# Layer 0 of a two-layer decoder: three products of 272 columns per weight chunk become products of 288, 256 and 272 columns, at changing places in memory

## The chip, the cores and the metric

The kernel runs on one core of a Trainium2 chip. Its engines each work through a queue of their own: TensorE (PE in the profile, with its weight loads as PEld), VectorE (DVE), ScalarE (ACT), GpSimd (POOL) and SyncE (SP), which issues DMAs. They wait for each other through semaphores. SBUF is the memory on the chip with 128 partitions; TensorE writes its sums to PSUM, in banks of 512 float32 columns. The metric is the device time of one execution in microseconds (us), as the median of several runs.

## The reference

256 tokens with 16 learned meta tokens in front (272 rows) go through two layers of width 2048, in float32. Cut to what matters here:

```python
h = concatenate([meta, x])                        # 272 x 2048
# layer 0
q, k, v, f = split(rms_norm(h) @ fox_w_in)        # 2048 -> 3*2048 + 16
h = h + forgetting_attention(q, k, v, cumsum(log_sigmoid(f + b))) @ fox_w_o
h = h + square(relu(rms_norm(h) @ w_up[0])) @ w_down[0]     # 2048 -> 8192 -> 2048
# layer 1
k_s, v_s = split(rms_norm(h, kv_norm) @ w_kv)     # all 272 rows
q = rms_norm(h) @ sb_w_q
h = h + stick_breaking_attention(q, k_s, v_s) @ sb_w_o
h = h + square(relu(rms_norm(h) @ w_up[1])) @ w_down[1]
return rms_norm(h, final_norm)[16:]
```

The meta tokens are needed up to the shared keys and values. From the queries of layer 1 on, only the 256 other tokens are computed.

## The kernel before

Everything is kept with the features on the partitions: `hT` is 128 partitions x 16 chunks x 272 tokens. A matrix product takes 128 x 128 weights as the stationary operand and a chunk of rows (128 features x tokens) as the moving one, in the type float32r. To keep float32's precision, both operands are split in two parts, a rounded one (`hi`) and the rest (`lo`), and three products are added up: weights-hi x rows-hi, weights-hi x rows-lo, weights-lo x rows-hi.

**Groups.** `gemm_group` (L186) makes 512 output features: 4 accumulators `acc` (one PSUM bank each, m = 0 to 3) by 4 blocks `kb` of the contraction, each with 4 chunks `kc`. A group is 4 x 16 x 3 = 192 products. For each `kb` the weights come by DMA into two tiles `raw` (L208, 512 KB each), ScalarE rounds them to `whi` (L220), VectorE subtracts to get `wlo` (L221). `whi` and `wlo` have 4 buffers each of half a block, so the splitting runs up to two blocks ahead. In the blocks 0 and 3 the products go accumulator by accumulator (12 in a row for each), in the blocks 1 and 2 half by half. At the end of block 3 a function `evac` takes each accumulator: in the projections VectorE multiplies it by the norm's factor (L377, L381), in the down and output products it adds it to `hT` (L255), in the up products it makes relu, square and split of it (L514 to L519). The next group uses the same four banks again.

**Stages.** Layer 0 has 12 groups for q, k and v (rows `a0`), 4 for the output product (`o0`), and for each of four quarters of the MLP 4 up groups (rows `m0`) and 4 down groups (rows `u0_0` to `u0_3`). Layer 1 begins with 4 groups for the queries on 256 tokens, then 8 groups for the shared keys and values on all 272 (rows `kv`); all that follows has 256 tokens. In the attention stages the small matrix products of the attention (L345 and others) are issued between the products of the groups.

**Where the rows lie.** `Split` (L119) holds `hi` and `lo` of one stage in one tile, 640 columns for each chunk. `ROWS` (L27) gives the first column of each: for 272 tokens `hi` at column 48 and `lo` at 368, for 256 tokens at 0 and 320. The tiles begin at a multiple of 64 columns (256 bytes), so that 48 and 368 are both column 48 of a stretch of 64. The weights lie at column 0 of their tiles where the rows are 272 and at column 16 where they are 256 (L212). In the layer-1 groups three products of each group are 262 columns wide instead of 256 (`wide`, L242 and L247); the six more columns are zeros and are not read.

**What sets the order.** The program is laid out by a scheduler that orders the instructions of each engine after a time model. The products of the groups are pinned one behind the other (`pinned`, L181). At the start, the first group loads the input and the weights by pieces, and takes the chunks one by one (L227).

Of the kernel before, what the change touches and what calls it, by code (L numbers as in the profile page):

```python
# [33 lines left out]
def yoco_kernel(ctx: ExitStack, tc: tile.TileContext, hT_in, gains, b_f, w_f, w_qkv0, w_o0, w_up, w_dn,  # L34
                w_kv, w_q1, w_o1, outT):
    nc = tc.nc
# [7 lines left out]
    tmp = ctx.enter_context(tc.tile_pool(name="tmp", bufs=2))  # L44
# [74 lines left out]
    class Split:  # L119


        def __init__(self, label, t0):
            n = T - t0
            self.t0 = t0
            rows = xs.tile([P, NC * XROW + 64], F32R, tag="x", name=f"x_{label}")
            hi, lo = ROWS[t0]
            rows = rows[:, hi:hi + NC * XROW].rearrange("p (c t) -> p c t", c=NC)
            d = lo - hi
            self.hi, self.lo = rows[:, :, :n], rows[:, :, d:d + n]
            if t0:  # L130

                self.wide = rows[:, :, :n + 6]
                nc.gpsimd.tensor_copy(rows[:, :, n:n + 6], pad[:, :6].unsqueeze(1).to_broadcast([P, NC, 6]))

    def split_chunk(sp, gi, c):

        g = g_sb[:, gi, c:c + 1]
        nc.scalar.activation(sp.hi[:, c], hT[:, c, sp.t0:], AF.Copy, scale=g)
        nc.vector.scalar_tensor_tensor(out=sp.lo[:, c], in0=hT[:, c, sp.t0:], scalar=g,
                                       in1=sp.hi[:, c].bitcast(F32), op0=ALU.mult, op1=ALU.subtract)  # L140

    class Norm:

# [34 lines left out]
    def gemm_matmul(*args, **kw):  # L178

        ins = nc.tensor.matmul(*args, **kw).ins  # L180
        if queued and pinned[0]:  # L181
            tc.add_manual_dep(ins, queued[0].name, mybir.DependencyInfo(mybir.DependencyClass.NoSync,
                                                                        mybir.DependencyReason.DATA))
        queued[:] = [ins]

    def gemm_group(wblk, sp, t0, evac, before={}, after={}, load_x=None):  # L186
# [4 lines left out]
        u = uid[0]  # L191
        accs = [pacc.tile([P, 512], F32, tag="acc", name=f"acc_{u}_{m}") for m in range(4)]
        n = T - t0
        for kb in range(4):
# [14 lines left out]
            parts = []  # L209
            for hf in range(2):  # L210
                whi, wlo = (wspl.tile([P, 2, 576], F32R, tag=f"w{x}", name=f"w{x}_{u}_{kb}_{hf}") for x in ("hi", "lo"))
                o = 16 if t0 else 0  # L212
                whi, wlo = whi[:, :, o:o + 512], wlo[:, :, o:o + 512]
                boxes = [(o, piece, 0, 512) for o in range(0, 2, piece)]
                if load_x is not None and kb == hf == 0:
                    boxes[:1] = [(0, 1, 0, 256), (0, 1, 256, 512)]
                for o, no, c0, c1 in boxes:
                    src = raws[hf][:, o:o + no, c0:c1]
                    hp, lp = whi[:, o:o + no, c0:c1], wlo[:, o:o + no, c0:c1]
                    on_act = nc.scalar.activation(hp, src, AF.Copy)  # L220
                    on_dve = nc.vector.tensor_tensor(out=lp, in0=src, in1=hp.bitcast(F32), op=ALU.subtract)  # L221
                parts.append((whi, wlo))
# [11 lines left out]
            for kcs, ms in runs:  # L234
                pairs = ((0, sp.hi), (0, sp.lo), (1, sp.hi))
                if t0:
                    products = [(kc, m, *pair) for pair in pairs for kc in kcs for m in ms]
                else:
                    products = [(kc, m, *pair) for m in ms for kc in kcs for pair in pairs]
                left = {m: 3 * len(kcs) for m in ms}  # L240

                wide = [(0, 0, 0), (1, 0, 1), (2, 1, 1)] if t0 else []  # L242
                for kc, m, part, x in products:
                    first, left[m] = kb == kc == 0 and left[m] == 3 * len(kcs), left[m] - 1
                    nw = n
                    if m == 3 and x is sp.hi and (kb, kc, part) in wide:
                        x, nw = sp.wide, n + 6  # L247
                    gemm_matmul(accs[m][:, :nw], parts[kc // 2][part][:, kc % 2, m * P:(m + 1) * P], x[:, 4 * kb + kc],
                                start=first, stop=kb == kc == 3 and left[m] == 0)
                if kb == 3:  # L250
                    for m in ms:
                        evac(m, accs[m][:, :n])

    def residual_add(c, acc, t0):
        nc.vector.tensor_tensor(out=hT[:, c, t0:], in0=acc, in1=hT[:, c, t0:], op=ALU.add)  # L255
# [109 lines left out]
    def put_split(sp, h, nh, t, n, src):  # L365
        hi, lo = (x[:, h:h + nh, t - sp.t0:t - sp.t0 + n] for x in (sp.hi, sp.lo))
        nc.scalar.activation(hi, src, AF.Copy)
        nc.vector.tensor_tensor(out=lo, in0=src, in1=hi.bitcast(F32), op=ALU.subtract)

    ao = Split("o0", 0)  # L370
    for g in range(4):
# [129 lines left out]
    def mlp(layer, xm, norm, t0, last_evac):  # L501
# [5 lines left out]
        for f in range(N_FF):  # L507
            u = Split(f"u{layer}_{f}", t0)
            for g in range(4):
                def evac(m, acc, g=g):  # L510
# [6 lines left out]
                    nc.scalar.activation(u.hi[:, c], u2[:, t0:], AF.Copy)  # L517
                    nc.vector.tensor_tensor(out=u.lo[:, c], in0=u2[:, t0:], in1=u.hi[:, c].bitcast(F32),
                                            op=ALU.subtract)  # L519
                gemm_group(w_up[layer, f, g], xm, t0, evac, {2: get_rstd} if f == g == 0 else {})  # L520
            for g in range(4):
                def evac(m, acc, g=g):
# [245 lines left out]
```

## Time and profile before

| | |
|---|---|
| median of 2 runs | 2295.25 us (2295.24 to 2295.26) |
| the profiled execution | 2294.73 us |
| its span, first to last instruction | 2293.0 us |
| PE busy | 2281.7 us, 19086 products |
| DVE, ACT, POOL busy | 1315.9, 1065.7, 39.8 us |
| mean granted clock of TensorE | 0.998 |

A line of the groups view names the line of the kernel, the engine, the operation, what is written and read with its shape, and the count; behind the bar stand the busy time, the mean duration of one in ns, and the idle time of the engine before it with what ended it. The duration of a product overlaps with the next one's, so what a product costs is read from the distance of starts. In the chain of waits and in the timeline, pieces that follow each other on one engine are merged: start, length, and how many.

### The profile page before, as it was taken

To read this page: it belongs to the slowest core of one execution; us is meant where nothing else is said; L and a number is where in the kernel's file an instruction comes from. 1 tells how busy PE (TensorE), PEld (TensorE's weight loads), DVE (VectorE), ACT (ScalarE), POOL (GpSimd) and SP (SyncE) were. 2 spreads that over 40 slices of the span, in tenths; PEclk is the share of its full clock that TensorE was granted. 3 is DMA by queue.
4 is the path that set the end of the run, shared out by engine and by line. 5 is a ranking of instruction groups with operands and counts; after the bars stand their busy time and mean duration, and the time that the engine had idled before them with its cause. 6 is when DMAs were issued, how large, how long until landed. Compare 5 with 4: busy or idle time off the path is not lost.

```text
span 2293.0 us, 45093 instructions
## 1 busy us (share of the span) xinstructions
PE 2281.7 (100%) x19086; PEld 2278.7 (99%) x19086; DVE 1315.9 (57%) x1834; ACT 1065.7 (46%) x1465; POOL 39.8 (2%) x65
## 2 busy tenths in 40 slices
PE   9999999999999999999999999999999999999998
PEld 9999999999999999999999999999999999999998
DVE  7666565654454455455566666666555555555555
ACT  6444444543354344344445555555544543543553
POOL 1000000000000000000000000000000000000000
PEclk9999999999999999999999999999999999999999
DMA  7544545555555555555555544456566556566563
GB/s 237 175 161 163 177 158 173 173 186 175 181 169 186 180 170 186 176 181 175 176 190 191 170 148 149 153 169 202 189 195 198 188 191 203 185 199 199 187 200 132
DMA packets 116906, 412.33 MB, mean 180 GB/s; under 512 B 13520, under 2 KB 16992, under 8 KB 116704
## 3 DMA queue, kind: packets, MB, share of 16 engines
q1 hardware_dynamic: 114560, 406.29, 53.3%
q8 instruction: 149, 2.44, 0.4%
q10 hardware_dynamic: 2144, 3.17, 0.4%
q14 instruction: 53, 0.43, 0.1%
HBM read 407.29 MB, written 2.11 MB: 179 GB/s over the span
## 4 chain that ended last, share of the span: by engine, by line
PE 99%; DVE 0%; DMA 0%; ACT 0%; SPq 0%; issue 0%; DVEq 0%; ACTq 0%
PE acc L180 96%; PE po L345 0%; PE pv L335 0%; PE ps L345 0%; PE pza L345 0%; DMA raw<-w_qkv 0%; PE po L655 0%; PE pzb L607 0%; PE ps L416 0%; PE po L483 0%; DVE ob L710 0%; PE pf L297 0%; PE pf L296 0%; PE pta L621 0%; PE pta L622 0%; PE pp L451 0%
## 5 line engine op out<-in xcount | busy, mean ns | idle before, releaser
L221 DVE TENSOR_TENSOR wlo<-raw,whi 128x1024 fp32r<-128x1024 f32 (+1 forms) x773 | 928.9, 1217 | 725.6 <-ACT whi L220 715.9
L220 ACT ACTIVATE whi<-raw 128x1024 fp32r<-128x1024 f32 (+1 forms) x773 | 797.3, 1050 | 966.7 <-PE acc L180 943.7
L180 PE MATMUL acc<-x_m,whi 128*128 128x272 f32 (+1 forms) x4096 | 643.0, 281 | 0.0
L180 PE MATMUL acc<-x_u,whi 128*128 128x272 f32 (+1 forms) x4096 | 642.5, 281 | 0.0
L180 PEld LDWEIGHTS acc<-x_m,whi 128*128 128x128 f32 x4096 | 565.9, 188 | 0.1
L180 PEld LDWEIGHTS acc<-x_u,whi 128*128 128x128 f32 x4096 | 565.7, 188 | 0.0
L180 PE MATMUL acc<-x_m,wlo 128*128 128x272 f32 (+2 forms) x2048 | 440.8, 281 | 0.0
L180 PE MATMUL acc<-x_u,wlo 128*128 128x272 f32 (+2 forms) x2048 | 440.8, 281 | 0.0
L180 PE MATMUL acc<-x_a,whi 128*128 128x272 f32 (+1 forms) x2048 | 357.9, 286 | 0.3 <-ACT whi L220 0.3
L180 PEld LDWEIGHTS acc<-x_m,wlo 128*128 128x128 f32 x2048 | 323.3, 188 | 0.0
L180 PEld LDWEIGHTS acc<-x_u,wlo 128*128 128x128 f32 x2048 | 323.3, 188 | 0.0
L180 PEld LDWEIGHTS acc<-x_a,whi 128*128 128x128 f32 x2048 | 301.5, 188 | 0.8 <-ACT whi L220 0.5
L180 PE MATMUL acc<-x_a,wlo 128*128 128x272 f32 (+2 forms) x1024 | 254.5, 286 | 0.0
L180 PE MATMUL acc<-x_kv,whi 128*128 128x272 f32 x1024 | 193.4, 288 | 0.0
L180 PEld LDWEIGHTS acc<-x_a,wlo 128*128 128x128 f32 x1024 | 175.5, 188 | 0.5 <-issue 0.5
L180 PE MATMUL acc<-x_o,whi 128*128 128x272 f32 (+1 forms) x1024 | 162.8, 282 | 0.0
L180 PEld LDWEIGHTS acc<-x_kv,whi 128*128 128x128 f32 x1024 | 160.0, 188 | 0.0
L180 PE MATMUL acc<-x_kv,wlo 128*128 128x272 f32 x512 | 146.8, 287 | 0.0
L180 PEld LDWEIGHTS acc<-x_o,whi 128*128 128x128 f32 x1024 | 142.2, 188 | 0.0
L255 DVE TENSOR_TENSOR hT<-acc,hT 128x272 f32<-128x272 f32 (+1 forms) x160 | 69.1, 432 | 81.7 <-PE acc L180 81.4
L180 PE MATMUL acc<-x_o,wlo 128*128 128x272 f32 (+2 forms) x512 | 110.9, 282 | 0.0
L180 PEld LDWEIGHTS acc<-x_kv,wlo 128*128 128x128 f32 x512 | 96.4, 188 | 0.1
(239 smaller groups left out, 1043.3 us busy)
## 6 DMA issues: line engine op xcount, KB each, us to landing
raw<-w_up SPq DMA_DIRECT2D x256, 512.0 KB, 4.4
raw<-w_dn SPq DMA_DIRECT2D x256, 512.0 KB, 4.5
raw<-w_qkv SPq DMA_DIRECT2D x92, 512.0 KB, 3.7
raw<-w_o SPq DMA_DIRECT2D x64, 512.0 KB, 4.3
raw<-w_kv SPq DMA_DIRECT2D x64, 512.0 KB, 3.7
raw<-w_q SPq DMA_DIRECT2D x32, 512.0 KB, 4.5
fk<-f_dram ACTq DMA_DIRECT2D x4, 544.0 KB, 4.7
raw<-w_qkv SPq DMA_DIRECT2D x7, 256.0 KB, 4.5
```

The source lines that it names most:

```text
L180: ins = nc.tensor.matmul(*args, **kw).ins
L220: on_act = nc.scalar.activation(hp, src, AF.Copy)
L221: on_dve = nc.vector.tensor_tensor(out=lp, in0=src, in1=hp.bitcast(F32), op=ALU.subtract)
L255: nc.vector.tensor_tensor(out=hT[:, c, t0:], in0=acc, in1=hT[:, c, t0:], op=ALU.add)
```

## The change

It changes the groups with 272 rows, that is all of layer 0 and the shared keys and values: 56 groups of 96.

- Each chunk of rows is laid out as 16 columns `meta`, then the 272 columns of `hi`, and further on the 272 columns of `lo`. `copy_meta` copies the first 16 columns of `lo` (those of the meta tokens) to `meta`, on GpSimd.
- The three products become: B, weights-hi x (`meta` and `hi`), 288 columns; A, weights-hi x `lo` without its first 16 columns, 256 columns; C, weights-lo x `hi`, 272 columns. B writes the columns 0 to 288 of the accumulator, A the columns 32 to 288, C the columns 16 to 288. The sum for the meta tokens is then in two parts, and ahead of each `evac` ScalarE copies the columns 0 to 16 and VectorE adds them to the columns 16 to 32.
- `PLACES` gives for each stage the column, within a stretch of 64, at which B and A begin (C begins 16 behind B). `form` gives for each group the column at which `whi` and `wlo` begin, and the order of A, B and C.
- The layer-1 groups with 256 rows keep their products and places.

```diff
-ROWS = {0: (48, 368), M: (0, 320)}
+ROWS = {M: (0, 320)}
+PLACES = {"a0": (0, 0), "o0": (32, 0), "m0": (48, 0), "u0_0": (0, 0), "u0_1": (48, 48), "u0_2": (0, 48),
+          "u0_3": (16, 0), "kv": (48, 32)}
+FOUR = [(0, 0, "BAC"), (16, 16, "BAC"), (0, 16, "BAC"), (16, 0, "BAC")]
+def form(u):
+    o = (0, 16, 32, 48)
+    if u <= 12:
+        return [(0, 0), (16, 16), (32, 32), (48, 48), (0, 16), (0, 32), (16, 0), (16, 32), (32, 0), (32, 16), (48, 0),
+                (0, 48)][u - 1] + ("BAC",)
+    if u <= 16:
+        return [(0, 0, "BAC"), (16, 16, "BAC"), (0, 0, "ACB"), (16, 16, "ACB")][u - 13]
+    if u <= 48:
+        f, g = divmod(u - 17, 8)
+        if g < 4:
+            return o[f], o[g], "BAC"
+        return [(0, 0, "ABC"), (0, 0, "BCA"), (0, 0, "CBA"), (16, 16, "ABC")][g - 4] if f == 0 else FOUR[g - 4]
+    if 53 <= u <= 60:
+        return ([*FOUR, (32, 32, "BAC"), (48, 48, "BAC"), (0, 48, "BAC"), (48, 0, "BAC")])[u - 53]
+    return 16, 16, ""
...
-            hi, lo = ROWS[t0]
+            hi, lo = ROWS[t0] if t0 else PLACES[label]
+            if not t0:
+                while lo < hi + n + 2 * M:
+                    lo += 64
+                lo -= M
...
+                self.meta, self.hi, self.lo = rows[:, :, :M], rows[:, :, M:M + n], rows[:, :, d:d + n]
+                self.form = {"A": (0, rows[:, :, d + M:d + n], 2 * M, M + n), "B": (0, rows[:, :, :M + n], 0, M + n),
+                             "C": (1, self.hi, M, M + n)}
...
+    def copy_meta(sp, c, n=1):
+        if sp.t0 == 0:
+            nc.gpsimd.tensor_copy(sp.meta[:, c:c + n], sp.lo[:, c:c + n, :M])
...
-                o = 16 if t0 else 0
-                whi, wlo = whi[:, :, o:o + 512], wlo[:, :, o:o + 512]
+                o1, o2, order = form(u)
+                whi, wlo = whi[:, :, o1:o1 + 512], wlo[:, :, o2:o2 + 512]
...
+                if not t0:
+                    for m in ms:
+                        for kc in kcs:
+                            for x in ("BAC" if kb == kc == 0 else order):
+                                part, rows, c0, c1 = sp.form[x]
+                                left[m] -= 1
+                                gemm_matmul(accs[m][:, c0:c1], parts[kc // 2][part][:, kc % 2, m * P:(m + 1) * P],
+                                            rows[:, 4 * kb + kc], start=kb == kc == 0 and x == "B",
+                                            stop=kb == kc == 3 and left[m] == 0)
+                    products = []
...
-                        evac(m, accs[m][:, :n])
+                        acc = accs[m][:, :n]
+                        if not t0:
+                            acc = accs[m][:, M:M + n]
+                            meta = tmp.tile([P, M], F32, tag="meta", name=f"meta_{u}_{m}")
+                            nc.scalar.copy(meta, accs[m][:, :M])
+                            nc.vector.tensor_tensor(out=acc[:, :M], in0=acc[:, :M], in1=meta, op=ALU.add)
+                        evac(m, acc)
```

`u` counts the groups in the order in which they run: 1 to 12 for q, k and v, 13 to 16 for the output product, 17 to 48 for the MLP (in eights, four up and four down), 49 to 52 for the queries of layer 1, 53 to 60 for the shared keys and values. `copy_meta` is called where a chunk's `hi` and `lo` are made: in `split_chunk`, in `put_split` for the meta tokens of the attention's output, and in the evacuation of the up products.

More of the change, by code (lines that the diff above doesn't have):

```diff
@@ L140, in split_chunk @@
                                        in1=sp.hi[:, c].bitcast(F32), op0=ALU.mult, op1=ALU.subtract)
+        copy_meta(sp, c)
     class Norm:
@@ L251, in gemm_group @@
                     for m in ms:
-                        evac(m, accs[m][:, :n])
+                        acc = accs[m][:, :n]
+                        if not t0:
+                            acc = accs[m][:, M:M + n]
[3 more added lines that the diff above has]
+                        evac(m, acc)
     def residual_add(c, acc, t0):
@@ L368, in put_split @@
         nc.vector.tensor_tensor(out=lo, in0=src, in1=hi.bitcast(F32), op=ALU.subtract)
+        if sp.t0 == t == 0 and n == M:
+            copy_meta(sp, h, nh)
     ao = Split("o0", 0)
@@ L519, in evac @@
                                             op=ALU.subtract)
+                    copy_meta(u, c)
                 gemm_group(w_up[layer, f, g], xm, t0, evac, {2: get_rstd} if f == g == 0 else {})
```

5 lines of the change are left out of this document (3 added, 2 removed).

## The prediction

> **What bounds the kernel now.** I read the page first (busy shares, slices, chain), then the chain of waits stretch by stretch, then the groups with shapes kept apart.
>
> ```profile
> span 2293.0 us, 45093 instructions
> PE 2281.7 (100%) x19086; PEld 2278.7 (99%) x19086; DVE 1315.9 (57%) x1834; ACT 1065.7 (46%) x1465; POOL 39.8 (2%) x65
> ...
> PEclk9999999999999999999999999999999999999999
> ...
> PE 99%; DVE 0%; DMA 0%; ACT 0%; SPq 0%; issue 0%; DVEq 0%; ACTq 0%
> ...
> L220 ACT ACTIVATE whi<-raw 128x1024 fp32r<-128x1024 f32 (+1 forms) x773 | 797.3, 1050 | 966.7 <-PE acc L180 943.7
> ```
>
> TensorE is busy for the whole span at full clock, the chain that ends last is 99% TensorE, and ScalarE, which makes the weights ready, waits 943.7 us for TensorE to give buffers back, not the other way round. So the time is the number of products times the distance from one start to the next. That distance stands in the chain, in two undisturbed stretches, the first of layer 0 (272 columns) and the second of layer 1 (256 columns, three of 192 with 262):
>
> ```profile
> 440.00 740.12 PE acc L180 x6001
> ...
> 1599.92 680.63 PE acc L180 x6000
> ```
>
> 740.12 / 6001 = 123.3 ns for 272 columns, 680.63 / 6000 = 113.4 ns for 256. Sixteen columns fewer are worth 9.9 ns, 0.62 ns a column, while the average over all 256 is 0.44 ns. Were the distance a fixed part and a part per column, 256 columns would leave no fixed part to speak of but a negative one (113.4 - 256 x 0.62 = -45 ns). So the distance is not linear; something steps up between 256 and 272. That is what the change can gain from, with the same 816 columns in three products.
>
> What the steps are worth is not constant either. The same products come in a second rhythm after a disturbance:
>
> ```profile
> 1195.80 1.11 PE L180 MATMUL acc<-x_a,wlo 128*128 128x256 f32 x8
> 1196.75 1.99 PE L180 MATMUL acc<-x_a,whi 128*128 128x256 f32 x16
> ...
> 70.63 0.42 PE L180 MATMUL acc<-x_a,whi 128*128 128x272 f32 x2
> ...
> 71.01 0.42 PE L180 MATMUL acc<-x_a,whi 128*128 128x272 f32 x2
> ...
> 71.39 0.42 PE L180 MATMUL acc<-x_a,whi 128*128 128x272 f32 x2
> ```
>
> From 1195.80 to 1196.75 eight products of 256 (the last of them 262) take 0.95 us, 118.8 ns each, and three products of 272 take 0.38 us from 70.63 to 71.01 and again to 71.39, 126.7 ns each. At the same sizes and places the distance is thus 113.4 or some 118.5, 123.3 or 126.7, with no wait that the profile shows. A product has a good and a bad rhythm, 3.4 to 5 ns apart.
>
> **The change part by part.** The groups with 272 rows are 56 x 192 = 10752 products, 3584 triples of 3 x 123.3 = 370.0 ns, together 1326 us. The 7680 products of layer 1 with 256 rows keep size, place and order and are costed at nothing; their cover is that no row of theirs is touched.
>
> *The triple.* C (272) stays between 123.3 and 126.7 ns. A (256) lies between 113.4 and 118.8. For B (288) the nearest rows are the attention's products of that width:
>
> ```profile
> 1496.45 0.13 PE pta L623
> 1496.58 0.14 PE pta L624
> 1496.72 0.13 PE ptb L626
> 1496.85 1.39 PE acc L180 x12
> 1498.23 0.23 PE po L345 x2
> ...
> L180 PE MATMUL acc<-x_m,whi 128*128 128x272 f32 x2048 | 379.3, 287 | 0.0
> ...
> L180 PE MATMUL acc<-x_m,whi 128*128 128x256 f32 x2032 | 261.9, 276 | 0.0
> ...
> L624 PE MATMUL pta<-el,nones_r 128*128 128x288 f32 x8 | 2.4, 296 | 0.0
> ```
>
> From 1496.45 to 1496.85 three take 0.40 us, 133.3 ns each; they read two pieces of 144 columns, at places that are not multiples of 16 columns, so I take that as B's upper end in the good rhythm. Its lower end is 288 at the cheapest rate per column seen, 288 x 113.4 / 256 = 127.6. The mean durations (276, 287, 296) say that the step from 272 to 288 is 9 ns after 11 from 256 to 272, which would be 123.3 + 9 = 132.3; the rate gives 127.6; I take 131, nearer to the row. The triple in good rhythm throughout is 131 + 113.4 + 123.3 = 367.7 ns, 2.3 ns less than today; in bad rhythm throughout, with B at 131 + 4, it is 135 + 118.8 + 126.7 = 380.5, 10.5 ns more.
>
> *The places.* The rows of one stage meet `whi` and `wlo` at columns 0, 16, 32 and 48 by turns, with one stage place for four to sixteen groups. In before all products of the groups stand in one relation: rows at 48 and weights at 0, or rows at 0 and weights at 16, in both 16 columns apart in a stretch of 64. No row shows the other relations for the groups. The nearest are the attention's products of 256 at other places: the two after 1498.23 take 0.23 us, some 117 ns, against 113.4. The change thus leaves for most groups the only relation in which the good rhythm is seen to hold; a gain from it cannot be excluded, since 123.3 itself may not be the best of 272. I charge each product between 0 and 3.6 ns (117 - 113.4), and take 1.0, since the good rhythm returned by itself in every stretch of 272: 367.7 + 3 x 1.0 = 370.7 ns, 0.7 ns more than now. Times 3584 that is +2.5 us. The ends are the per-column rate for all three (816 x 0.443 = 361.5 ns, -8.5 ns, -30 us) and bad rhythm throughout (+10.5 ns, +38 us).
>
> The Trainium skill, "TensorE: Matmul & The Clock Gate", section "Back-to-back issue gap", has a warm product at its columns over 2.4 plus about 2.5 ns. By it 272 columns would take 115.8 ns and any three products with 816 columns 347.5, before and after alike, so the sizes would be worth nothing. The rows differ from it in both ways: 123.3 is 7.5 ns more, and the distance is not linear in the columns. The same page of the Trainium skill ("Step-by-step: what each phase is for") says that loading the next weights takes nothing from the moving operand's reads, by which the places of the weights would not matter; no run so far varies them alone.
>
> *The order of A, B and C* (ACB, ABC, BCA, CBA in six groups) changes which product follows which; cost 0, within the bounds of the places.
>
> *The additions.* 224 times ScalarE copies 16 columns out of an accumulator and VectorE adds them before the evacuation, and GpSimd makes 116 copies of `meta`.
>
> ```profile
> L367 ACT ACTIVATE x_o<-pom 128x64 fp32r<-128x64 f32 x4 | 0.9, 223 | 1.5 <-PE pom L476 1.5
> ...
> L362 POOL COPY pk_sm<-s 128x64 f32<-128x64 f32 x8 | 1.8, 237 | 132.5 <-PE acc L180 132.5
> ...
> 2282.87 0.17 DVE fin L691
> ...
> L221 DVE TENSOR_TENSOR wlo<-raw,whi 128x1024 fp32r<-128x1024 f32 (+1 forms) x773 | 928.9, 1217 | 725.6 <-ACT whi L220 715.9
> ...
> L255 DVE TENSOR_TENSOR hT<-acc,hT 128x272 f32<-128x272 f32 (+1 forms) x160 | 69.1, 432 | 81.7 <-PE acc L180 81.4
> ```
>
> The copy is some 0.22 us, the addition 0.17, GpSimd's copy 0.24. What hides them is the time until the bank is used again: 36 products of the other three accumulators, 36 x 0.123 = 4.4 us. The chain is copy, addition, evacuation, 0.22 + 0.17 + 0.43 = 0.82 us; with a split of weights ahead of it on each of the two engines (1.05 and 1.22) it is 3.1 us. Behind the waiting copy on ScalarE stand the next splits of weights, and for those TensorE would wait; but ScalarE's 943.7 us of idle time say that they are made as soon as a buffer is free. Cost 0. If the cover were gone, each 0.5 us of lateness in a group costs 56 x 0.5 = 28 us.
>
> *The start.* B needs `hi`, `lo` and `meta` of the first chunk, where the first product took `hi` alone.
>
> ```profile
> 4.57 0.52 ACT L138 ACTIVATE x_a<-hT,g_sb 128x272 fp32r<-128x272 f32 x1
> ...
> 5.13 0.52 DVE L139 SCALAR_TENSOR_TENSOR x_a<-hT,g_sb,x_a 128x272 fp32r<-128x272 f32 x1 [0.22 <-ACT x_a L138]
> 5.14 0.78 PEld L180 LDWEIGHTS acc<-x_a,whi 128*128 128x128 f32 x5
> ...
> 0.00:33.00 33.00, 31.57 (x237) 30.80 (x238) 27.73 (x52) 27.56 (x55) 5.58 (x24) 1.00 0.86 292
> ```
>
> The first product moves from 5.14 to 5.65 plus GpSimd's copy, 5.9: +0.8 us. GpSimd is still at its masks there (5.58 us busy in this stretch), and each of the 16 chunks has one more hand-over, of which TensorE's 1.4 idle us show that few decide. I take +2, between 0 and 4.
>
> *Moved tiles.* The new `meta` buffers push the attention's tiles on by 128 bytes. The attention's 192 two-part products change their places; at most 5 ns each, 1 us; taken as 0.
>
> Sum: 2294.7 + 2.5 + 2 = 2299.2 for the profiled execution; the median stood 0.5 us above it, so about 2300 us.
>
> **The rivals.**
>
> *Columns alone count.* If a triple costs what its columns cost, only the start is left: 2295.25 + 2 = 2297 us. For it: layer 0 holds 123.3 over 6001 products whatever the other engines do. Against it: 113.4 for 256.
>
> *The step is gone.* If 272 pays for something that products of mixed sizes do not meet, all three go at 0.443 ns a column: 361.5 ns, -30 us, and +2 for the start: 2267 us. For it: layer 1 holds that rate over 6000 products. Against it: C is still 272 columns wide, and 288 at 133.3 ns in the attention pays more than that rate. Faster by over 2% (more than 46 us, 12.8 ns a triple) would need 357 ns, a rate that no row has.
>
> *The bad rhythm stays (slower).* Layer 1 leaves it at a product of 262 columns (at 1196.75 the next 16 take 1.83 us, 114.4 each); layer 0 has no such product, before or after. In a relation in which the bad rhythm is the stable one, a group keeps it: 118.8 + 126.7 + 133.3 + 4 = 382.8 ns, +12.8, +46 us, with the start 2343 us. It decides from 4.3 ns a product, averaged over the 56 groups. For it: four relations for each pair of rows and weights where one was, and both rhythms are in the trace. Against it: 272 always fell back to 123.3.
>
> *The evacuation comes late.* Price above; it needs more than 4.4 us against 3.1, and would show as idle time of TensorE that is now zero.
>
> **How the numbers follow.** Forecast, good and bad rhythm mixed: 0.50, its own range 2283 to 2322 us. Columns alone: 0.17. The step is gone: 0.14, a third of it beyond 2%. The bad rhythm stays: 0.17, two thirds of it beyond 2%. Late evacuation: 0.02. The range, 2262 to 2345 us, reaches from the step gone to the bad rhythm and leaves out 0.05 below and 0.11 above. Two per cent is about what a measurement of this kernel is taken to tell from no change. Faster by over 2%: 0.05; slower by over 2%: 0.12; within: 0.83.
>
> **What would show it.** In the chain, an undisturbed stretch of layer 0 should have 123 to 125 ns for each product, in steps from group to group where the places change; the shapes kept apart should show 288 some 8 to 12 ns over 272. Layer 1 from 1600 us on should keep 113.4. TensorE's idle time should grow by no more than 4 us, all of it at the start. I am wrong if groups with equal sizes differ by more than 5 ns a product, if all groups run below 121, or if TensorE waits for accumulators.

## The result and the profile after

The changed kernel takes 2320.9 us (2320.7 to 2321.1, 2 runs) against 2295.25: the ratio is 1.011, with a 95% interval of 1.0094 to 1.0127. It is slower by 25.65 us, inside 2%. The forecast was 2300, so the sign and the class were right and the size was 21 us short. The page of the changed kernel, first the span and the busy shares, then the chain that ended last, then groups of instructions:

```profile
span 2319.0 us, 45824 instructions
PE 2301.0 (99%) x19086; PEld 2296.1 (99%) x19086; DVE 1353.3 (58%) x2058; ACT 1098.6 (47%) x1689; POOL 61.8 (3%) x181
...
PE 97%; DVE 1%; DMA 0%; ACT 0%; POOL 0%; issue 0%; SPq 0%; DVEq 0%; ACTq 0%
...
L258 ACT ACTIVATE whi<-raw 128x1024 fp32r<-128x1024 f32 (+1 forms) x773 | 798.8, 1053 | 853.4 <-PE acc L218 824.2
L304 ACT COPY meta<-acc 128x16 f32<-128x16 f32 x224 | 37.4, 167 | 152.3 <-PE acc L218 146.6
```

The count of products is the same, 19086. The span is 26.0 us longer (2319.0 - 2293.0). TensorE's busy time grew by 19.3 us (2301.0 - 2281.7), so its idle time grew by 6.7. The bound is still TensorE: ScalarE still waits 824.2 us for it to give the weights' buffers back. The line L304 is the new copy, 167 ns each.

Both parts are to be found by stage. The chain's pieces of the product line within single groups, and one from layer 1 (start, length, how many; the length divided by the count is the distance from start to start):

```profile
510.91 22.16 PE acc L218 x178
...
604.95 23.14 PE acc L218 x183
...
652.88 23.19 PE acc L218 x188
...
677.94 22.10 PE acc L218 x176
...
1648.98 651.02 PE acc L218 x5739
```

They are groups 20, 24, 26 and 27: 124.5, 126.4, 123.4 and 125.6 ns a product, as a mean over the three sizes. Times three that is, within the rounding of such a piece, 373.3, 380, 370 and 376.7 ns a triple. No group of the MLP averages below 370 or above 380. Most groups, once settled, stand on one of these four levels, which are 3.3 ns apart; some lie between them, as group 31 at 374.7 and group 35 at 377.9. The last line is layer 1: 651.02 / 5739 = 113.4 ns, as before.

The MLP of layer 0, first before and then after, in the view of the busy time in a window (the window, its length, the busy time of PE, PEld, DVE, ACT and POOL with counts, the granted clock, the DMA share, GB/s):

```profile
424.00:1182.00 758.00, 758.00 (x6146) 757.92 (x6146) 396.81 (x484) 326.75 (x419) 0.27 (x1) 1.00 0.53 178
```

```profile
436.50:1204.00 767.50, 767.50 (x6147) 767.42 (x6146) 420.02 (x613) 343.56 (x547) 13.53 (x67) 1.00 0.53 176
0.00:38.00 38.00, 32.45 (x243) 31.23 (x243) 28.44 (x57) 27.74 (x58) 19.97 (x40) 1.00 0.80 272
```

The same 6146 products take 767.5 instead of 758.0 us, TensorE is busy in all of both, the clock is 1.00 in both, and the DMA share is 0.53 in both. That is 9.5 / 6146 = 1.5 ns a product, without any idle time. The second line after is the start, up to the second group: TensorE idles 5.55 us in it (38.00 - 32.45), where it idled 1.43.

Where it waits, by the view of PE's waits (engine and line, who was waited for: us in total, times, longest):

```profile
PE acc L218 <- POOL x_a L170: 4.4, 2, 3.2
...
PE acc L218 <- DVE qT L433: 1.0, 3, 0.3
PE acc L218 <- ACT x_o L421: 0.7, 1, 0.7
PE ps L399 <- DVE x_o L422: 0.6, 1, 0.6
PE ps L472 <- DVE kT L437: 0.5, 1, 0.5
```

All five are new. The first is at the start: a product waits for GpSimd's copy of 16 columns. The two waits of the score product `ps` are in the attention stage, where it needs an evacuated k (`x_o` holds its two parts there). The three waits for `qT` are of another kind: in the groups 5, 8 and 11 the first product on the fourth accumulator waits for VectorE to evacuate that accumulator. The wait for ScalarE's `x_o` is in the first output group of layer 1. From the starts of the groups in the two traces, the 26.0 us divide like this:

| stage | later by, us |
|---|---|
| start, up to group 2 | 4.4 |
| groups 2 to 12 with the attention | 6.1 |
| output product | 1.8 |
| MLP of layer 0 | 9.4 |
| queries of layer 1, then shared keys and values | 0.1 + 2.4 |
| first output group of layer 1 | 1.2 |
| rest of layer 1, tail | 0 + 0.6 |

So three causes had to be told apart: what the places cost, what the sizes cost, and what the additions at the start and at the evacuation cost.

### The profile page after: what moved, and what is told of

The parts are those of the page before. It is cut to its first block, busy times and chain, and to the rows that moved or that the text cites. A ratio compares the mean times of both kernels' runs of the same rounds, so it can differ in the third digit from the quotient of the medians.

```text
span 2319.0 us, 45824 instructions
## 1 busy us (share of the span) xinstructions
PE 2301.0 (99%) x19086; PEld 2296.1 (99%) x19086; DVE 1353.3 (58%) x2058; ACT 1098.6 (47%) x1689; POOL 61.8 (3%) x181
## 4 chain that ended last, share of the span: by engine, by line
PE 97%; DVE 1%; DMA 0%; ACT 0%; POOL 0%; issue 0%; SPq 0%; DVEq 0%; ACTq 0%
PE acc L218 94%; PE po L399 0%; DMA raw<-w_qkv 0%; DVE wlo L259 0%; POOL x_a L170 0%; PE pv L389 0%; DVE s L457 0%; PE pza L399 0%; ACT whi L258 0%; PE ps L399 0%; PE po L712 0%; PE pzb L664 0%; PE po L539 0%; PE ps L472 0%; DVE ob L767 0%
## 5 line engine op out<-in xcount | busy, mean ns | idle before, releaser
L258 ACT ACTIVATE whi<-raw 128x1024 fp32r<-128x1024 f32 (+1 forms) x773 | 798.8, 1053 | 853.4 <-PE acc L218 824.2
L218 PE MATMUL acc<-x_u,whi 128*128 128x256 f32 (+1 forms) x4096 | 647.4, 282 | 0.0
L218 PE MATMUL acc<-x_m,whi 128*128 128x256 f32 (+1 forms) x4096 | 647.2, 282 | 0.0
L218 PE MATMUL acc<-x_a,whi 128*128 128x256 f32 (+1 forms) x2048 | 360.5, 287 | 5.5 <-POOL x_a L170 4.4
L218 PE MATMUL acc<-x_kv,whi 128*128 128x288 f32 (+1 forms) x1024 | 196.6, 289 | 0.0
L218 PE MATMUL acc<-x_o,whi 128*128 128x256 f32 (+1 forms) x1024 | 164.5, 283 | 0.7 <-ACT x_o L421 0.7
L304 ACT COPY meta<-acc 128x16 f32<-128x16 f32 x224 | 37.4, 167 | 152.3 <-PE acc L218 146.6
```

What stands on the lines that cost most here:

```text
L304: nc.scalar.copy(meta, accs[m][:, :M])
```

## The experiments

The times of before, run beside these on the same chips, have medians of 2294.97 to 2295.9 us. Where one time is given without an interval, it is from one execution.

**One: the start.** In the changed kernel, VectorE makes the copies of the meta columns for the first stage, GpSimd the others.

```diff
...
-            nc.gpsimd.tensor_copy(sp.meta[:, c:c + n], sp.lo[:, c:c + n, :M])
+            eng = nc.vector if sp.label == "a0" else nc.gpsimd
+            eng.tensor_copy(sp.meta[:, c:c + n], sp.lo[:, c:c + n, :M])
```

> The changed kernel with one edit: the copies of the meta columns of the first stage (rows a0, 16 of them) are made by VectorE instead of GpSimd. If the first group's 4.4 us come from GpSimd's copies (0.9 us each there, 0.2 elsewhere, with TensorE waiting 4.4 us for them), the time falls by 2.5 to 4.5 us, to 2316.5 to 2318.5, and the second group starts between 33.6 and 35.5 us instead of 38.0. If the first group is late because its first product needs the lo part at all, whoever copies, the time falls by less than 1 us.

Measured: 2317.88 us (2317.27 to 2318.37), ratio 1.0097 (1.0081 to 1.0114); the interval overlaps that of the change, so 3.0 us is the difference of the medians and no more. The groups view of the changed kernel has the copies on GpSimd, by the stage that they belong to:

```profile
L170 POOL CAST x_a<-x_a 128x16 fp32r<-128x16 f32 x16 | 14.4, 901 | 8.9 <-DVE x_a L176 8.9
L170 POOL CAST x_u<-x_u 128x16 fp32r<-128x16 f32 x64 | 12.6, 196 | 659.1 <-DVE x_u L574 659.1
```

The same view of the experiment:

```profile
L171 DVE CAST x_a<-x_a 128x16 fp32r<-128x16 f32 x16 | 2.5, 172 | 0.0
```

The same copy takes 901 ns at the start and 196 in the MLP, and 172 on VectorE. The prediction had charged 240 from a copy of 64 columns. The time is as expected. The wait for GpSimd is gone, but the second group begins at 36.07 us, later than expected and not at 33.6 as before: so of 4.4 us 1.9 come back, and a wait of 0.7 for VectorE's `x_a` remains. GpSimd's copies were thus a part of the delay, less than half. VectorE has 2.5 us more to do in that stage now; whether the rest of the delay comes from that is not shown.

**Two: one place.** All groups of the changed kernel get the same places, B at 48 (so C at 64, which is 0) and A at 0, the weights at 16, and the order BAC. Sizes, copies and additions stay.

```diff
-PLACES = {"a0": (0, 0), "o0": (32, 0), "m0": (48, 0), "u0_0": (0, 0), ...
+PLACES = dict.fromkeys(("a0", "o0", "m0", "u0_0", "u0_1", "u0_2", "u0_3", "kv"), (48, 0))
...
-    o = (0, 16, 32, 48)
...
+    if u <= 48 or 53 <= u <= 60:
+        return 16, 16, "BAC"
```

> The changed kernel with all 56 groups at one place (B at column 48, A and C at 0, weights hi and lo at 16) and one order, BAC: the place of group 26, whose triple took 370 ns. Places theory: every triple of an undisturbed stretch takes 370 ns as three products of 272 did, the MLP of layer 0 takes 758 us instead of 767.6, and the time is 2302 to 2308 us (start and idle time of the changed kernel are left). Sizes theory (288, 256 and 272 in turn cost more than 3 x 272 wherever they lie): the triple stays at 374 to 376 ns and the time between 2316 and 2322.

Measured: 2306.62 us (2305.6 to 2311.54), ratio 1.0053 (1.0038 to 1.0068). The chain from the end of group 13 into group 17, then through the MLP from group 18 on:

```profile
354.93 90.90 PE acc L206 x724
445.82 0.46 PE pms_m L187 x2
...
479.96 710.15 PE acc L206 x5758
```

710.15 / 5758 = 123.33 ns, 370.0 a triple, in one undisturbed piece: exactly what three products of 272 columns took before. By the starts of the groups the MLP takes 9.2 us less than in the change, so nearly all of the 9.4 us it had lost is the price of the places.

The first line shows that a place alone doesn't fix the rate. With the same places, sizes and order, 90.90 / 724 = 125.6 ns, 376.7 a triple, through the output product and into group 17, where before had 123.3. Only behind the two products `pms_m` of the norm does it change to 370.0, where it stays to the end of the MLP. So in the good rhythm the sizes cost nothing and bring nothing, but here the mixed sizes also have a slower one that lasts.

Of the 14.3 us, 2.7 come from the start: the second group begins at 35.27 us instead of 38.00, and GpSimd's copies for the first stage take 454 ns each instead of 901. The groups view:

```profile
L158 POOL CAST x_a<-x_a 128x16 fp32r<-128x16 f32 x16 | 7.2, 454 | 11.6 <-DVE x_a L164 11.6
```

Why they are faster here is not known.

**Three: the places of the weights alone.** The kernel before, with its three products of 272 columns and its rows, but the weights placed by group as in the change.

```diff
...
-                o = 16 if t0 else 0
-                whi, wlo = whi[:, :, o:o + 512], wlo[:, :, o:o + 512]
+                o1, o2, _ = form(u)
+                whi, wlo = whi[:, :, o1:o1 + 512], wlo[:, :, o2:o2 + 512]
```

> The kernel before (three products of 272, rows at column 48) with one edit: the weights hi and lo lie at the columns that the change gives them, group by group, 0, 16, 32 or 48. Places theory, if the weights' places count by themselves: the groups differ, between 123.3 and 126.7 ns a product, with the groups at 0 and 0 staying at 123.3, and the time is 2300 to 2315 us. If the weights' places matter only beside the mixed sizes, or not at all: 123.3 in all groups and 2295 us.

Measured: 2318.75 us, 23 us over before. The chain in groups 22 and 26:

```profile
553.95 21.09 PE acc L200 x171
...
649.00 23.05 PE acc L200 x182
```

Group 22 has its weights at 0, as before, and keeps 21.09 / 171 = 123.3 ns. Group 26 has them at 16 and takes 126.6. Nothing else differs between them and the same groups of before, so the place of the weights alone sets the distance of starts of products whose rows stayed where they were. The loss was larger than expected; the places of the weights on their own cost almost as much as the whole change.

**Four: is it the place, or the relation?** As experiment three, with the rows of each stage moved too.

```diff
-ROWS = {0: (48, 368), M: (0, 320)}
+ROWS = {M: (0, 320)}
+PLACES = {"a0": (32, 32), "o0": (16, 48), "m0": (0, 0), "u0_0": (16, 16), "u0_1": (0, 32), "u0_2": (32, 0),
+          "u0_3": (48, 16), "kv": (0, 16)}
...
```

> As the run before it with weights at changing places and three products of 272, and the rows of each stage at another place too (hi and lo: a0 32 and 32, m0 0 and 0, u0_0 16 and 16, u0_1 0 and 32, u0_2 32 and 0, u0_3 48 and 16). Relation theory: only the distance of weights from rows within a stretch of 64 columns counts, so in m0 the group with weights at 16 and 16 (distance 16, as rows 48 and weights 0) takes 123.3 ns a product and those at 0 and 0 or 32 and 32 take 125 to 127; in u0_0, rows 16, the groups at 0 and 0 take 126.7. Absolute theory (the weights' or the rows' place by itself): weights at 0 and 0 keep 123.3 wherever the rows are. Time 2312 to 2322 us either way.

Measured: 2317.08 us. The chain in groups 17, 22 and 26:

```profile
425.89 16.77 PE acc L204 x134
...
553.97 20.14 PE acc L204 x159
...
649.99 21.09 PE acc L204 x171
```

Groups 22 and 26 have changed roles. Group 22 has rows at 16 and weights at 0: 126.7 ns. Group 26 has rows at 0 and weights at 16: 123.3. Group 17, both at 0, takes 125.1. What counts is the difference of the two columns within a stretch of 64 (weights minus rows): 16 gives 123.3; 0 gives some 125.3; 32 and 48 give 126.7, in the MLP groups of these two runs. All groups of before stand at a difference of 16.

**Five: the additions alone.** The kernel before, with GpSimd's copies (to columns that no one reads), and a copy and an addition ahead of each evacuation. ScalarE multiplies by zero, so the sums stay what they were.

```diff
...
-                        evac(m, accs[m][:, :n])
+                        acc = accs[m][:, :n]
+                        if not t0:
+                            meta = tmp.tile([P, M], F32, tag="meta", name=f"meta_{u}_{m}")
+                            nc.scalar.activation(meta, acc[:, :M], AF.Copy, scale=0.0)
+                            nc.vector.tensor_tensor(out=acc[:, :M], in0=acc[:, :M], in1=meta, op=ALU.add)
+                        evac(m, acc)
```

> The kernel before with the additions of the change and none of its products: GpSimd copies the 16 meta columns (to columns that no product reads), and ahead of each evacuation ScalarE makes 16 columns (times zero) from the accumulator and VectorE adds them. Places theory and sizes theory alike: hidden, 2295 to 2297 us. Additions theory (the longer way out of the accumulator, or its place in the queues, delays TensorE): 2300 to 2310 us, above all in the attention stage, where the changed kernel has 2.1 us of new idle time of TensorE and 6.1 us in all.

Measured: 2301.07 us (2299.59 to 2304.16), ratio 1.0024 (1.0014 to 1.0035), 5.4 us over before. By the starts of the groups, 5.1 us have accrued by group 13, 3.4 of them in group 3, and the MLP adds 0.0. Group 3 in the windows view, before:

```profile
59.80:87.10 27.30, 27.30 (x224) 27.30 (x223) 22.36 (x64) 13.51 (x32) 0.43 (x2) 1.00 0.52 174
```

And with the additions, first the window, then PE's waits:

```profile
59.70:90.30 30.60, 28.59 (x229) 28.03 (x228) 24.20 (x72) 15.02 (x38) 0.44 (x2) 1.00 0.47 157
```

```profile
PE ps L356 <- DVE x_o L379: 1.8, 1, 1.8
...
PE acc L186 <- DVE qT L390: 1.0, 3, 0.3
...
PE ps L429 <- DVE kT L394: 0.3, 1, 0.3
```

Where a group lasted 27.30 us without a gap, it lasts 30.60 with 2.01 us idle. The waits name two reasons. In group 3 it is the score product `ps`, which reads the evacuated k: it comes sooner than the 36 products in which the prediction hid the chain.

The waits for `qT` are at the bank. The groups 4 to 6, 7 to 9 and 10 to 12 take 0.6 us more each, and in each of the three this wait is the only one. The timeline around the start of group 5 at 118.09 us, by engine:

```profile
117.43 2.01 ACT L226 ACTIVATE whi<-raw 128x1024 fp32r<-128x1024 f32 x2 [0.44 <-PE acc L186]
119.34 0.16 ACT L261 ACTIVATE meta<-acc 128x16 f32<-128x16 f32 x1
...
120.61 1.22 DVE L227 TENSOR_TENSOR wlo<-raw,whi 128x1024 fp32r<-128x1024 f32 x1
...
122.03 0.17 DVE L262 TENSOR_TENSOR acc<-acc,meta 128x16 f32<-128x16 f32 x1
...
122.53 0.43 DVE L390 SCALAR_TENSOR_TENSOR qT<-acc,rstd_a 128x272 f32<-128x272 f32 x1
...
123.01 0.52 PE L186 MATMUL acc<-x_a,whi 128*128 128x272 f32 x2 [0.32 <-DVE qT L390]
```

ScalarE's copy stands behind two splits of weights, and VectorE's addition behind splits and the decays of the scores. So the evacuation ends 4.9 us after the start of group 5, and the product that needs this bank, 36 products or 4.4 us after that start, waits.

**Six: the sizes.** The kernel before, with all products of an MLP group of layer 0 in one width, another width for each group. Where the width is under 272, the last tokens are left out of those products; the first product on each accumulator keeps 272.

```diff
+SIZES = (256, 260, 264, 268, 272, 276, 280, 284, 288, 256, 260, 264, 268, 272, 280, 288)
...
+                    if 17 <= u <= 48:
+                        nw = max(SIZES[(u - 17) % 16], n if first else 0)
+                        x = sp.wides[x is sp.lo][:, :, :nw]
```

> The kernel before, rows and weights at its places, but in the 32 MLP groups of layer 0 all three products have one width, another in each group: 256, 260, 264, 268, 272, 276, 280, 284, 288, and again. Widths under 272 leave out the last tokens, so the output is not the reference's there. Step theory (a step between 256 and 272): 113 to 118 ns up to some width, then a jump of several ns, then 0.42 ns a column, 288 at 130. Slope theory (0.62 ns for each column past 256): 115.8, 118.3, 120.8, 123.3, 125.8, 128.3, 130.8, 133.3 for 260 to 288. The additions of the change are not in it.

The time (2303.28 us) says nothing here; the chain does, in groups of 256, 264, 268, 272, 280, 284 and 288 columns, in this order (264 from the second quarter of its group on, where it has settled; 260 and 276 are read in the same way):

```profile
647.98 14.05 PE acc L186 x124
...
476.93 15.12 PE acc L186 x126
...
496.00 21.01 PE acc L186 x166
...
518.89 21.21 PE acc L186 x172
...
564.89 25.15 PE acc L186 x196
...
592.96 21.07 PE acc L186 x158
...
617.89 22.13 PE acc L186 x166
```

| columns | 256 | 260 | 264 | 268 | 272 | 276 | 280 | 284 | 288 |
|---|---|---|---|---|---|---|---|---|---|
| ns | 113.3 | 120.0 | 120.0 | 126.6 | 123.3 | 126.7 | 128.3 | 133.4 | 133.3 |

The distance is a staircase, and not a rising one: 268 columns cost more than 272. 256, 272, 280 and 288 lie on a line of 10 ns for 16 columns, so 113.3 + 123.3 + 133.3 = 370.0 = 3 x 123.3, to the tenth. Neither theory stood as it was put: the line holds for these four widths and not for the others.

**Seven: a second rhythm.** The kernel before with its weights at 48 for `whi` and 0 for `wlo`, and in each MLP group one product wider by 0, 2, 4 ... 30 columns of zeros that are not read.

```diff
+def kick(u):
+    return 2 * ((u - 17) % 16) if 17 <= u <= 48 else 0
...
+                    if not t0 and (kb, kc, m, part) == (0, 0, 3, 0) and x is sp.hi:
+                        x, nw = sp.wide, n + kick(u)
+                        x = x[:, :, :nw]
```

> The kernel before with weights hi at 48 and lo at 0 in all groups with 272 rows: the relation that in the run with changing places of the weights took 126.7 ns a product in one MLP group and 122.2 in the last group of the shared keys and values, after attention work had come between. In the MLP groups of layer 0 one product of each group (first chunk, last accumulator) is 0, 2, 4 to 30 columns wider, on zeros that are not read. Two-rhythms theory: some widenings switch a group from 126.7 to 122.2 and others switch it back, at the same places; the MLP groups then lie at two or more levels, and which one follows from the widening. One-rate theory (the relation alone sets the rate, and the last group was special for its stage): all MLP groups stay at 126.7 whatever the widening.

Measured: 2318.98 us. The chain in group 20, and in group 21 behind its product of 280 columns:

```profile
504.93 21.15 PE acc L187 x167
...
532.90 16.13 PE acc L187 x132
```

126.6 ns, then 16.13 / 132 = 122.2. By the starts in the trace the slow rhythm goes on through the first 36 products of group 21, so nothing but that one product, 8 columns wider, lies between the two. In group 22 the next wider product (+10) ends it. It comes again in group 37 with the same width, and in groups 27 and 43 (+20); in the attention stages, too, some groups run at 122.2 and others at 126.7. So at these places the same instructions have two rhythms, each of which lasts until something disturbs it, and the better one is below the 123.3 of before.

**Eight: one wider product to switch it.** As seven, but the weights at these places only from group 18 on, and only group 18 with a product of 280.

```diff
-    return 2 * ((u - 17) % 16) if 17 <= u <= 48 else 0
+    return 8 if u == 18 else 0
...
```

> The kernel before with two edits: in the groups 18 to 48 (the MLP of layer 0 but its first group) the weights hi lie at 48 instead of 0 (lo stay at 0), and one product of group 18 is 280 columns wide instead of 272, on zeros that are not read. Two-rhythms theory: the groups enter in the slow rhythm (126.7 ns a product) and the wider product switches them to 122.2, which then holds for the 31 groups; 31 x 64 triples x 3.3 ns = 6.6 us less than before, 2288 to 2290 us. If the rhythm falls back at each change of rows or weights, or the wider product does not switch from this entry: 126.7 ns in all of them, +20 us, 2315 us.

Measured: 2314.75 us (2314.48 to 2315.77), ratio 1.0083 (1.0068 to 1.0099). The chain from group 21 on:

```profile
529.93 640.17 PE acc L187 x5054
```

126.67 ns over 5054 products: it did not switch. So the width alone doesn't decide whether the rhythm switches.

**Nine: one place, and the start on VectorE.** Experiments two and one together.

```diff
+            eng = nc.vector if sp.label == "a0" else nc.gpsimd
+            eng.tensor_copy(sp.meta[:, c:c + n], sp.lo[:, c:c + n, :M])
...
+PLACES = dict.fromkeys(("a0", "o0", "m0", "u0_0", "u0_1", "u0_2", "u0_3", "kv"), (48, 0))
...
```

> The changed kernel with both edits tried before: one place and one order for all groups, and the first stage's meta copies on VectorE. If places and start are separate terms, their savings of 14.3 and 3.0 us add: 2302.5 to 2304.5 us, which leaves about 8 us over the kernel before, of which the additions alone took 5.4. If the first group's wait is taken over by the next wait: 2305 to 2307 us.

Measured: 2305.4 us (2305.1 to 2307.9), ratio 1.0044 (1.0029 to 1.0058), 1.2 us below experiment two with overlapping intervals. PE's waits:

```profile
PE ps L388 <- DVE x_o L411: 1.4, 1, 1.4
...
PE acc L207 <- DVE x_a L159: 0.8, 1, 0.8
```

The two gains did not add, since experiment two had most of the start's gain already: its second group began at 35.27 us with GpSimd's copies, and begins at 36.33 here with VectorE's. The wait for GpSimd is gone, a wait for VectorE's `x_a` stands in its place, and the score product waits 1.4 us for `x_o` where it waited 0.6 in the change; the same 1.4 stands in experiment one.

**Ten: one place, a bad one.** Experiment two with B at 32 instead of 48, and so C at 48 instead of 0.

```diff
-PLACES = dict.fromkeys(("a0", "o0", "m0", "u0_0", "u0_1", "u0_2", "u0_3", "kv"), (48, 0))
+PLACES = dict.fromkeys(("a0", "o0", "m0", "u0_0", "u0_1", "u0_2", "u0_3", "kv"), (32, 0))
```

> The changed kernel with all groups at one place again, but with B at column 32 instead of 48 (C at 48 instead of 0; A at 0, weights at 16 as in the run with one place): the place of the groups 14 and 16, whose triple took 380 ns. Places theory: 380 ns a triple in all undisturbed groups, 10 ns more than with B at 48, in all 30 to 36 us over that run: 2337 to 2343 us. If groups 14 and 16 were slow for another reason (their stage, the attention before them): 370 to 376 ns and 2307 to 2328 us.

Measured: 2333.64 us, 27 us over experiment two. The chain through the MLP:

```profile
479.95 710.09 PE acc L206 x5606
```

126.67 ns a product, 380 ns a triple, in all MLP groups. The difference in the triple is the 10 ns expected; the total came out a little lower than expected, since the groups ahead of the MLP stood at 123.7 to 125.6 ns in experiment two already.

**Eleven and twelve: two wider products, and one.** Experiment eight, with group 19 wider by 6 and group 20 by 8, as in the scan ahead of its switch; and with group 19 alone wider by 8.

```diff
-    return 8 if u == 18 else 0
+    return {19: 6, 20: 8}.get(u, 0)
```

> As the run with one wider product, but the wider products stand where the scan had them: 6 more columns in one product of group 19, 8 more in one of group 20, after group 18 has settled. The slow rhythm repeats every two triples, and in the scan the 8 columns switched it only where they met the second triple of the two, the 6 columns of the group before having moved it by one. Phase theory: the groups 21 to 48 and most of 20 take 122.2 ns a product, the groups 18 and 19 126.7; 29 x 64 triples x 3.3 ns less and 2 x 64 x 10 ns more, 4.9 us less than before: 2290 to 2292 us. Otherwise 126.7 ns throughout and 2315 us.

The second of them:

```diff
-    return 8 if u == 18 else 0
+    return {19: 8}.get(u, 0)
```

> The same with the 8 more columns alone, in group 19. Phase theory: they meet the first triple of the two and do not switch; 126.7 ns a product in the groups 18 to 48 and 2315 us. If 8 columns switch from any settled slow rhythm (the run with one wider product failed because it was not settled): 122.2 ns from group 20 on, 2290 us.

Measured with two: 2291.54 us (2290.08 to 2292.67, 11 runs), ratio 0.9981 (0.9972 to 0.999). With one: 2315.4. The chain with two, in groups 18 and 19, and from group 21 on:

```profile
452.00 43.07 PE acc L187 x340
...
529.90 640.20 PE acc L187 x5238
```

With one:

```profile
479.92 700.09 PE acc L187 x5527
```

43.07 / 340 = 126.7, then 640.20 / 5238 = 122.22 ns to the end of the MLP; with one wider product 126.67 throughout. The version with two is faster than both kernels. The sum fits: groups 21 to 48 are 28 x 192 products by 1.11 ns less, -6.0 us, and groups 18 and 19 cost 384 x 3.34 = +1.3, together -4.7 against -3.9 measured. Two products with 14 more columns between them, instead of one with 8, make a difference of 23.9 us.

Both came out as the phase theory had it, and the starts of single products in the traces agree with it. In the run with one wider product the slow rhythm repeats over two triples: 127, 126, 125, then 125, 131, 126 ns from start to start. Group 19 there, where 8 columns did not switch it, begins with the first of these triples. The groups in which 8 columns did switch it (21 and 37 of the scan, 20 of the run with two) begin with the second. That is four cases; no run moved the phase alone.

## Why the prediction was right, and where it was not

The class held with room to spare and not by exactness: the sum put 4.5 us on the profiled execution where 26.0 were measured.

*The bound.* Right. The time remained the number of products times the distance of starts, and layer 1 kept its 113.4 ns.

*The sizes.* B was put at 131 ns, between two ends; it is 133.3 (experiment six), the end from the attention's row of 288 columns, although those rows lie elsewhere in memory. The good triple is 370.0 and not 367.7 (experiment two). The gain of 2.3 ns that the prediction set against the places was not there. The groups view of the changed kernel, shapes apart, shows the order of the three only roughly, as the ends are modelled:

```profile
L218 PE MATMUL acc<-x_m,whi 128*128 128x288 f32 x1024 | 301.6, 294 | 0.0
L218 PE MATMUL acc<-x_m,wlo 128*128 128x272 f32 x1024 | 294.2, 287 | 0.0
```

Seven nanoseconds between 272 and 288 in the mean duration, where the prediction looked for 8 to 12; the distance of starts has 10.

*The places.* The term was seen and undersized. It was taken at 1.0 ns a product because "the good rhythm returned by itself in every stretch of 272". That step failed: the good rhythm returned where every group of before stood, at a difference of 16 columns; at others it does not (experiments three and four). In the MLP it costs 1.5 ns a product, 4.6 a triple, where sizes and places together had been put at 0.7. The reason is that it isn't one price for all: some groups pay nothing (370), some the full 10 ns (380), and a group that has settled keeps its price. Which price a place gets is not fixed by the place alone: experiment two has 376.7 and 370.0 at the same one. The rival of a bad rhythm that stays was thus right in its mechanism, for a part of the groups: with all of them at 380 in the MLP, experiment ten took 2333.64.

The Trainium skill, "TensorE: Matmul & The Clock Gate", section "Step-by-step: what each phase is for", says that loading the next weights doesn't take read bandwidth from the running product. Experiment three speaks against building on it here: with the rows in their place and only the weights' columns moved, 123.3 became 126.6 ns. Whether it is the reads that collide, these runs don't show.

*The order of A, B and C.* Costed at 0, and it was 0: the groups 13 and 15, which differ in the order alone, both settle at 373.3 ns, and 14 and 16 both at 380.

*The additions.* Costed at 0, in error: 5.4 us (experiment five). The cover named, 36 products until the bank is used again, holds in the MLP, which adds 0.0. Ahead of it the cover fails twice. The prediction looked for the next writer of the bank only, not for the next reader of the rows, and the scores wait for k. And in the groups 5, 8 and 11 the bank itself comes too late, by 0.3 us each: more stands ahead of the addition in the queues than the one split of weights on each engine that made up the 3.1 us.

*The start.* Forecast +2 us, between 0 and 4; it was +4.4. The first product began at 6.00 us, as reckoned (5.9); the delay arose at the chunks behind it. The item that was mis-sized for certain is GpSimd's copy, 0.24 us in the sum, 0.90 in the trace; with VectorE's copies 1.9 of the 4.4 us came back, and where the rest arises is open. The Trainium skill, "SBUF — State Buffer", section "Who interferes with whom", has a VectorE instruction with two inputs in SBUF contend with a GpSimd instruction that reads there; VectorE makes the `lo` parts from two such inputs at that time, and the slow copies agree with that. But the same copies took 454 ns in experiment two, and no run took VectorE's work away to show it.

*The marks.* Layer 0 in steps from group to group: right, though up to 126.7 rather than 125 ns. Equal sizes within 5 ns: right, 3.3 at most. TensorE's idle time up by no more than 4 us, all at the start: wrong, 6.7, and by the waits 1.1 us lie at the scores, 1.0 at the accumulators of the groups 5, 8 and 11, and 0.7 in the first output group of layer 1. So one of the signs of being wrong did show: TensorE waited for accumulators.

*The rivals.* "Columns alone count" would have had 2297; its triple of 370.0 is right at good places, but by a staircase that happens to meet a line at 256, 272 and 288. "The step is gone" is refuted by 133.3 for 288. The evacuation did come late, at the scores and, in three groups, at the bank; and the additions cost 5.4 us in all. The formula of columns over 2.4 plus 2.5 ns that the prediction drew on stands in the Trainium skill, "TensorE: Matmul & The Clock Gate", section "Back-to-back issue gap", for an isolated product, not for a stream of weight loads and products; the stream measured here took 123.3 ns at 272 columns against its 115.8.

## What to carry to other kernels

When a stream is bound by TensorE, read the distance of starts group by group: a loss that no wait shows can be the columns at which rows and weights begin, and one run with a single place for all groups helps to tell it from the sizes; look in that run, too, for stretches that keep different distances. Before work is put ahead of an evacuation, ask for the first reader of the result, not only for the next writer of the buffer, and add up what stands ahead of it in each engine's queue. A price per column read from two widths says nothing of the widths between them.

## What the runs showed of the hardware

- The distance of starts depends on the difference of the columns at which weights and rows begin, within a stretch of 64 columns (256 bytes): 123.3 ns at 16, some 125.3 at 0, 126.7 at 32 and 48, for 272 columns with both parts of the weights at one place. With three products of different widths and differences, no simple sum over the three was found: in the change, group 26 has A and C at 16 and B at 32 and takes 370 ns, group 24 has A and B at 16 and C at 0 and takes 380.
- More columns can take less time: 268 at 126.6, 272 at 123.3.
- At one and the same place, the stream can have two lasting rhythms: 122.2 and 126.7 ns for 272 columns (experiments seven, eleven and twelve), 123.3 and 125.6 ns a product for the three sizes of the change (experiment two). A product that is a few columns wider can switch between them, and need not: one of 280 columns did in the scan (group 21), and did not in experiments eight and twelve.

Open are the cause of the steps in the hardware, what exactly makes a wider product switch the rhythm (whether the 8 columns in group 20 would do without the 6 in group 19 was not tried), whether the better rhythm can be had in the attention stages too, and why GpSimd's copies at the start took 901 ns in the change and 454 in experiment two.
